# Expert 0's first weight loads ahead of the rank registers, and one 128-slot chunk beside every three 64-slot chunks

## The chip, the cores and the metric

The kernel runs on one core of a Trainium2 chip. The metric is the time of one execution on the device, in microseconds; the median of three runs before the change is 1743.07 us (1742.59 to 1744.09). In the rows PE is TensorE's matmul side and PEld its weight loads, DVE is VectorE, ACT is ScalarE, and SPq is the sequencer of SyncE, which issues all DMA transfers in the order of the program.

## The reference

Two layers of a diffusion backbone over 256 latent tokens of width 1024. Each layer has four token mixers, an output projection and a feed-forward part. In layer 0 that part is a dense SwiGLU; in layer 1, where the change lies, each token goes to two of eight experts:

```python
def swiglu(h, w_gate, w_up, w_down):
    return (jax.nn.silu(h @ w_gate) * (h @ w_up)) @ w_down

def moe_swiglu(h, router_w, w_gate, w_up, w_down):
    ...
    logits = (t @ router_w).astype(jnp.float32)
    top_val, top_idx = lax.top_k(logits, TOP_K)
    top_w = jax.nn.softmax(top_val, axis=-1)
    gate = jnp.sum(jax.nn.one_hot(top_idx, N_EXPERTS, dtype=jnp.float32) * top_w[..., None], axis=1)
    for e in range(N_EXPERTS):
        out = out + gate[:, e:e + 1] * swiglu(t, w_gate[e], w_up[e], w_down[e]).astype(jnp.float32)
```

The hidden width is 3584 and all is in float32. An expert's three matrices are 44 MB, the eight together 352 MB, and every execution reads all of them from the chip's main memory.

## The kernel before

The last stage computes the eight experts from gathered tokens. Each expert has a fixed number of places for tokens (slots). Expert 0 has 128. The seven others are put in order of their load at run time: the fullest, rank 0, gets 128 slots as well, and ranks 1 to 6 get 64 each. Tokens beyond that would go through a loop behind a branch (line 1450).

An expert's hidden width is cut into 14 chunks of 256. A chunk needs three units of weights, 128 x 2048 floats (1 MiB) each: two for the gate and up projections (tile gu) and one for the down projection (tile yd with 128 slots, ys with 64). Each unit is one DMA, issued by `raw_unit` (line 228, or two half transfers in line 223). `raw_unit` walks through a ring of twelve buffers: the old context tile (x), one spare tile, the old parameter tile (prb), a pair of half tiles (cst and prb), and eight raw tiles. A transfer waits until its buffer's last reader is done, and what stands behind it on the queue waits too.

The two kinds of experts are computed in different ways. A 128-slot chunk (`full`) splits each half unit into a high part by ACT (`wh`, line 235) and a remainder by DVE (`wl`, line 237), and PE takes three matmuls in the place of one (`mm3`, lines 245 to 247). There are three pairs of split tiles, and a raw buffer is free when DVE has made the remainder. A 64-slot chunk (`small`) lets PE read the raw buffer as it is (line 1394 for gu, line 1380 for ys), with two halves of the array side by side. In both, ACT applies silu (lines 1332 and 1397), and the down projection of a chunk is computed one chunk later.

Where an expert's weights lie depends on its rank, so seven register loads on SP (line 1436) fetch the order from the tile `ordi`, which DVE writes at the end of the routing. Expert 0's addresses are known when the program is built. Four of its units are loaded during attention (line 1076), and its first four chunks (`HEAD`) stand ahead of everything else.

Behind these, `prep_small` gathers the tokens of ranks 1 to 3 (tile es) and `prep_full` those of rank 0 (tile ef). The loop of lines 1440 to 1447 then runs over the 84 chunks of the 64-slot experts and puts one 128-slot chunk ahead of each for as long as there are any: expert 0's last ten, then the 14 of rank 0. Ranks 4 to 6 are prepared at step 20. A scheduler orders each engine's instructions from this program, with its own model of time.

Of the kernel before, what the change touches and what calls it, by code (L numbers as in the profile page):

```python
# [22 lines left out]
NCH = 14  # L23
# [161 lines left out]
def build(tc, I, out):  # L185
    nc = tc.nc
# [12 lines left out]
    turns = {"raw": 0, "split": 0, "unit": 0}  # L199
# [5 lines left out]
    def ring(kind):  # L205
        i = 2 if kind == "raw" else 3
        n = turns[kind] % sum(w[i] for w in wps)
        turns[kind] += 1
        for w in wps:
            if n < w[i]:  # L210
                return w[0], w[i]
            n -= w[i]

    more = []

    def raw_unit(src, n=2048):
        turns["unit"] += 1
        i = turns["unit"] % (len(more) + sum(w[2] for w in wps))
        if i < len(more):
            r = more[i]()  # L220
            if isinstance(r, list):
                for k, h in enumerate(r):
                    nc.sync.dma_start(h, src[:, k * 1024:k * 1024 + 1024])
                return r
        else:
            wp, bufs = ring("raw")
            r = wp.tile([128, n], F32, tag="raw", bufs=bufs, name="raw")
        nc.sync.dma_start(r, src)
        return r

    def split(r):
# [12 lines left out]
    def mm3(o, wh, wl, rh, rl, start, stop, **kw):  # L244
        PE.matmul(o, wh, rh, start=start, stop=False, **kw)  # L245
        PE.matmul(o, wh, rl, start=False, stop=False, **kw)  # L246
        PE.matmul(o, wl, rh, start=False, stop=stop, **kw)  # L247

    def hilo(hi, lo, src):
        S.activation(hi, src, AF.Copy)  # L250
        V.tensor_tensor(out=lo, in0=src, in1=hi.bitcast(F32), op=ALU.subtract)
# [34 lines left out]
    def adav(l, j, kt, s):  # L286
        return ada[l][:, j * 8 + kt, s:s + 1]
# [16 lines left out]
    def t8(name, dt=F32R, shape=(128, 8, 256)):  # L304
        return a8.tile(list(shape), dt, tag="a8", name=name)
# [10 lines left out]
    def t2(name, shape=(128, 2, 256), dt=F32):  # L316
        return tt("t2", name, shape, dt)
# [426 lines left out]
    def PS():  # L744
        turn[0] += 1
        return PB() if turn[0] % 5 > 2 else pq.tile([128, 512], F32, tag="b0", bufs=3, name="b0")
# [303 lines left out]
    def masks(gm, slots, numbers="iota"):  # L1050

        for t in range(2):
            for i, sl in enumerate(slots):
                j = V.tensor_scalar(gm[:, t, i], C(numbers), sl[t], None, op0=ALU.is_equal)
        return j.ins
# [102 lines left out]
    NR = NE - 1  # L1158
    cap = sm.tile([128, 8], F32, tag="cap", bufs=1, name="cap")
    slr = sm.tile([128, 4, NR], F32, tag="slr", bufs=1, name="slr")  # L1160
    cnti = sm.tile([128, 2], I32, tag="cnti", bufs=1, name="cnti")
    ordi = sm.tile([128, NR], I32, tag="ordi", bufs=1, name="ordi")
# [57 lines left out]
    def slots_of(st, gm, gates):  # L1220

        st.gT = gp.tile([128, 256], F32R, tag="gT", name="gT")
        st.g = sm.tile([128, 1], F32, tag="sg", bufs=8, name="sg")
        ps = PS()
        for t in range(2):
            PE.transpose(ps[:, t * 128:t * 128 + 128], gm[t], ident)
        for t in range(2):
            PE.matmul(ps[:, 256:257], gm[t], gates[t], start=t == 0, stop=t == 1)
        S.activation(st.gT, ps[:, :256], AF.Copy)
        V.tensor_copy(st.g, ps[:, 256:257])  # L1230

    def gather(gm, kts, ps, n):
        for i, kt in enumerate(kts):
            for t in range(2):
                PE.matmul(ps[:, i * n:i * n + n], ht[:, t, kt * 128:kt * 128 + 128], gm[t], start=t == 0, stop=t == 1)

    def prep_full(slots, gates, gm=None):

        st = St()
        if gm is None:  # L1240
            gm = t2("gm", (128, 2, 1, 128))
            masks(gm, [slots])
        gm = [gm[:, t, 0] for t in range(2)]
        e = t8("ef", F32R, (128, 2, 8, 128))
        for k4 in range(2):
            ps = PS()
            gather(gm, range(4 * k4, 4 * k4 + 4), ps, 128)
            for k in range(4):
                kt = 4 * k4 + k
                sh = adav(1, 3, kt, 0)  # L1250
                S.activation(e[:, 0, kt], ps[:, k * 128:k * 128 + 128], AF.Identity, bias=sh)
                V.scalar_tensor_tensor(e[:, 1, kt], ps[:, k * 128:k * 128 + 128], sh, e[:, 0, kt].bitcast(F32), op0=ALU.add,
                                       op1=ALU.subtract)
        st.e = (e[:, 0], e[:, 1])
        slots_of(st, gm, gates)
        return st
# [30 lines left out]
    def split_unit(e, u):  # L1287
        if isinstance(e, int) and e == 0 and u in first:
            r = first[u]
            ws = []  # L1290
            for a in (0, 1024):
                nsplit[0] += 1
                with ExitStack() as st:
                    if nsplit[0] > EARLY:
                        st.enter_context(tc.issue_after(last_mask))
                        st.enter_context(tc.issue_after(sbi))
                    ws.append(split(r[:, a:a + 1024]))
            return ws
        return halves(unit_at(e, u))

    def full(st, e):

        yd = []

        def down(c, g):
            if not yd:
                yd.extend(pq.tile([128, 512], F32, tag=f"yd{i}", name=f"yd{i}") for i in range(2))
            pt = pq.tile([128, 512], F32, tag="tr", bufs=2, name="tr")
            for m in range(2):
                PE.transpose(pt[:, m * 128:m * 128 + 128], g[:, m * 128:m * 128 + 128], ident)  # L1310
            hhl = t2("hhl", (128, 2, 256), F32R)
            hh, hl = hhl[:, 0], hhl[:, 1]
            hilo(hh, hl, pt[:, :256])
            for m, wd in enumerate(split_unit(e, c * 3 + 2)):
                for q in range(2):
                    a = slice(q * 512, q * 512 + 512)
                    h = slice(m * 128, m * 128 + 128)
                    mm3(yd[q], hh[:, h], hl[:, h], wd[0][:, a], wd[1][:, a], c == 0 and m == 0, c == NCH - 1 and m == 1)

        prev = []  # L1320

        def chunk(c):
            eh, el = st.e
            ps = pq.tile([128, 512], F32, tag="gu", bufs=2, name="gu")
            for hf in range(2):
                for k2, w in enumerate(split_unit(e, c * 3 + hf)):
                    for k in range(2):
                        kt = 4 * hf + 2 * k2 + k
                        a = slice(k * 512, k * 512 + 512)
                        mm3(ps, eh[:, kt], el[:, kt], w[0][:, a], w[1][:, a], kt == 0, kt == 7)  # L1330
            g = t1("sg")
            S.activation(g, ps[:, :256], AF.Silu)
            V.tensor_tensor(out=g, in0=g, in1=ps[:, 256:], op=ALU.mult)
            if c:
                down(c - 1, prev.pop())
            prev.append(g)
            if c == NCH - 1:
                down(c, prev.pop())
                st.y = t8("y", F32R, (128, 2, 1024))
                for q in range(2):  # L1340
                    a = slice(q * 512, q * 512 + 512)
                    S.activation(st.y[:, 0, a], yd[q], AF.Copy, scale=st.g)
                    V.scalar_tensor_tensor(st.y[:, 1, a], yd[q], st.g, st.y[:, 0, a].bitcast(F32), op0=ALU.mult,
                                           op1=ALU.subtract)
                scatter_full(st)

        return [lambda c=c: chunk(c) for c in range(NCH)]
# [79 lines left out]
        st0 = prep_full(None, [gate[:, t, 0:1] for t in range(2)], gm0)  # L1427
    more[:] = [old] + [lambda r=r: r for r in spares[:NPRE]] + [old2, old3]
    turns["unit"] = len(more) - 1
    turns["split"] = turns["raw"] = 0  # L1430
    A = full(st0, 0)
    HEAD = 4
    for f in A[:HEAD]:
        f()
    more[:] = [old, lambda: spares[0], old2, old3]
    order = [nc.values_load(ordi[0:1, r:r + 1], engines=(mybir.EngineType.SP,), min_val=1, max_val=7) for r in range(NR)]
    small_sts = prep_small([1, 2, 3])
    st1 = prep_full([slr[:, 2 * t + 1, 0:1] for t in range(2)], [slr[:, 2 * t, 0:1] for t in range(2)])
    A = A[HEAD:] + full(st1, order[0])
    for i in range(6 * NCH):  # L1440
        if i == NCH + 6:
            small_sts += prep_small([4, 5, 6])
        if i < len(A):
            A[i]()
        if i % NCH == 0:
            B = small(small_sts[i // NCH], order[i // NCH + 1], i // NCH == 5)
        B[i % NCH]()
    over = nc.values_load(cnti[0:1, 0:1], min_val=0, max_val=1024)

    with tc.If(over > 512):  # L1450
# [42 lines left out]
```

## Time and profile before

| | us |
|---|---|
| median of the runs (lowest to highest) | 1743.07 (1742.59 to 1744.09) |
| the profiled execution | 1743.34 |
| its span, first to last instruction | 1741.5 |
| PE, matmuls, busy | 1642.9 |
| DVE busy | 856.1 |
| ACT busy | 645.5 |

The page has 525.25 MB of transfers, a mean of 302 GB/s over the span. Its second part cuts the span into 40 equal slices of 43.5 us; a digit is the busy share in tenths. The expert stage begins near 850 us, that is, half-way through these lines.

### The profile page before, as it was taken

What the parts mean: (1) busy time and instruction counts of PE and PEld (TensorE: products, weight loads), DVE (VectorE), ACT (ScalarE), POOL (GpSimd) and SP (SyncE); (2) the same over time, 40 slices, a digit from 0 to 9 for tenths busy, and PEclk for the clock granted to TensorE, in tenths of its full rate; (3) what the DMA queues carried; (4) which work ended last, traced back from release to release, by engine and by line L of the source; (5) the groups of instructions that cost most, each with busy time, mean ns of one, the idle gap of its engine ahead of it and who ended that gap; (6) DMA issues with size and microseconds to landing.
All of it is one profiled execution on the core that took longest, in us unless ns stands there. A gap on an engine that the chain in (4) does not pass through costs nothing.

```text
span 1741.5 us, 28675 instructions
## 1 busy us (share of the span) xinstructions
PE 1642.9 (94%) x11648; PEld 1245.3 (72%) x11648; DVE 856.1 (49%) x1446; ACT 645.5 (37%) x1026; POOL 32.1 (2%) x31
## 2 busy tenths in 40 slices
PE   7999999999999999999999999999999887888886
PEld 4897899999999999989775566566655443444443
DVE  3546676797666666566665555555541110110101
ACT  4534564444454444455664444444430000000000
POOL 0100000000000000000100000000000000000000
PEclk9999999999999999999999999999999999999999
DMA  9425456777644666654579999999999999999997
GB/s 377 158 96 194 141 199 225 291 271 303 245 153 165 222 253 241 224 217 168 199 278 377 381 359 386 390 350 398 381 367 415 419 418 419 418 419 418 420 418 289
DMA packets 77900, 525.25 MB, mean 302 GB/s; under 512 B 9024, under 2 KB 9152, under 8 KB 18240
## 3 DMA queue, kind: packets, MB, share of 16 engines
q1 hardware_dynamic: 77760, 523.33, 77.0%
q8 instruction: 94, 1.54, 0.3%
q14 instruction: 46, 0.38, 0.1%
HBM read 522.25 MB, written 1.05 MB: 300 GB/s over the span
## 4 chain that ended last, share of the span: by engine, by line
PE 73%; DMA 21%; DVE 3%; ACT 2%; issue 1%; POOL 0%; SPq 0%; DVEq 0%; ACTq 0%; POOLq 0%
DMA raw<-in_moe 13%; PE gu L246 9%; PE gu L245 9%; PE gu L247 9%; PE gu L1394 8%; DMA prb<-in_moe 4%; PE acc L246 4%; PE acc L245 4%; PE acc L247 4%; PE ys L1380 3%; DMA x<-in_moe 2%; PE w L245 2%; PE w L247 2%; PE w L246 2%; PE yd L246 1%; PE yd L245 1%
## 5 line engine op out<-in xcount | busy, mean ns | idle before, releaser
L237 DVE TENSOR_TENSOR wl<-raw,wh 128x1024 fp32r<-128x1024 f32 x304 | 370.0, 1224 | 187.8 <-ACT wh L235 181.9
L235 ACT ACTIVATE wh<-raw 128x1024 fp32r<-128x1024 f32 x304 | 319.9, 1059 | 304.8 <-PE gu L246 148.0
L1394 PE MATMUL gu<-raw,es 128*64 128x256 f32 x2048 | 256.8, 385 | 33.3 <-DMA raw<-in_moe 33.3
L245 PE MATMUL gu<-fh,wh 128*128 128x256 f32 x896 | 254.1, 284 | 0.0
L247 PE MATMUL gu<-fh,wl 128*128 128x256 f32 x896 | 251.3, 281 | 0.0
L246 PE MATMUL gu<-fl,wh 128*128 128x256 f32 x896 | 250.9, 280 | 0.0
L1394 PEld LDWEIGHTS gu<-raw,es 128*64 128x64 f32 x2048 | 144.8, 136 | 120.4 <-issue 39.5
L1397 ACT ACTIVATE sg<-gu 64x256 f32<-64x256 f32 x84 | 31.7, 377 | 427.1 <-PE gu L1394 426.6
L1398 DVE TENSOR_TENSOR sg<-sg,gu 64x256 f32<-64x256 f32 x84 | 35.7, 425 | 276.5 <-ACT sg L1397 275.9
L245 PEld LDWEIGHTS gu<-fh,wh 128*128 128x128 f32 x896 | 168.1, 188 | 4.7 <-issue 4.7
L246 PEld LDWEIGHTS gu<-fl,wh 128*128 128x128 f32 x896 | 168.6, 188 | 2.7 <-issue 2.7
L247 PEld LDWEIGHTS gu<-fh,wl 128*128 128x128 f32 x896 | 168.8, 189 | 1.8 <-issue 1.6
L246 PE MATMUL acc<-hl,wh 128*128 128x256 f32 x448 | 124.5, 283 | 0.0
L245 PE MATMUL acc<-hh,wh 128*128 128x256 f32 x448 | 123.8, 283 | 0.0
L247 PE MATMUL acc<-hh,wl 128*128 128x256 f32 x448 | 120.3, 283 | 0.0
L1380 PE MATMUL ys<-raw,hs 128*64 128x512 f32 x400 | 96.0, 599 | 14.8 <-DMA raw<-in_moe 14.0
L246 PE MATMUL gu<-wl,ef 128*128 128x512 f32 x224 | 93.1, 415 | 3.8 <-DVE wl L237 3.7
L245 PE MATMUL gu<-wh,ef 128*128 128x512 f32 x224 | 92.2, 412 | 0.0
L247 PE MATMUL gu<-wh,ef 128*128 128x512 f32 x224 | 88.0, 393 | 0.0
L246 PEld LDWEIGHTS acc<-hl,wh 128*128 128x128 f32 x448 | 85.7, 191 | 0.0
L245 PEld LDWEIGHTS acc<-hh,wh 128*128 128x128 f32 x448 | 85.6, 191 | 0.0
L247 PEld LDWEIGHTS acc<-hh,wl 128*128 128x128 f32 x448 | 83.3, 191 | 0.0
(450 smaller groups left out, 2549.4 us busy)
## 6 DMA issues: line engine op xcount, KB each, us to landing
raw<-in_moe SPq DMA_DIRECT2D x223, 1024.0 KB, 12.3
raw<-in_ffn SPq DMA_DIRECT2D x84, 1024.0 KB, 4.8
spare<-in_moe SPq DMA_DIRECT2D x31, 1024.0 KB, 10.4
x<-in_moe SPq DMA_DIRECT2D x28, 1024.0 KB, 12.6
prb<-in_moe SPq DMA_DIRECT2D x27, 1024.0 KB, 8.7
rx<-in_ada SPq DMA_DIRECT2D x19, 1024.0 KB, 5.0
raw<-in_ada SPq DMA_DIRECT2D x18, 1024.0 KB, 4.9
prb<-in_moe SPq DMA_DIRECT2D x27, 512.0 KB, 10.1
```

The lines of the kernel that those rows point to most:

```text
L235: S.activation(hi, r, AF.Copy)
L237: V.tensor_tensor(out=lo, in0=r, in1=hi.bitcast(F32), op=ALU.subtract)
L245: PE.matmul(o, wh, rh, start=start, stop=False, **kw)
L246: PE.matmul(o, wh, rl, start=False, stop=False, **kw)
L247: PE.matmul(o, wl, rh, start=False, stop=stop, **kw)
L1380: PE.matmul(yd[0][64 * q:64 * q + 64, :], h[:, m * 64:m * 64 + 64], rs[m][:, q * 512:q * 512 + 512], start=c == 0 and m == 0, stop=c == NC ...
L1394: PE.matmul(ps[64 * q:64 * q + 64, :256], st.e[:, kt], rs[k // 2][:, a:a + 256], start=kt == 0, stop=kt == 7, tile_position=(0, 64 * q))
L1397: S.activation(g[64:], ps[:64, :256], AF.Silu)
L1398: V.tensor_tensor(out=g[64:], in0=g[64:], in1=ps[64:, :256], op=ALU.mult)
```

## The change

The diff does two things. The register loads are placed behind the issue of the last weight transfer of the four head chunks (`newest`), and the ring of raw buffers starts at another place. And the loop turns round: every step has its 64-slot chunk, and every third step adds one 128-slot chunk from the list A; rank 0 is prepared at step 28, where expert 0's chunks end, and ranks 4 to 6 at step 36. With 24 chunks in the list, the last 128-slot chunk now goes with step 71 of 0 to 83; before it went with step 23.

```diff
-        nc.sync.dma_start(r, src)
+        newest[:] = [nc.sync.dma_start(r, src).ins]
...
-    turns["split"] = turns["raw"] = 0
+    turns["split"], turns["raw"] = 0, 3
...
-    order = [nc.values_load(ordi[0:1, r:r + 1], engines=(mybir.EngineType.SP,), min_val=1, max_val=7) for r in range(NR)]
+    with tc.issue_after(newest[0]):
+        order = [nc.values_load(ordi[0:1, r:r + 1], engines=(mybir.EngineType.SP,), min_val=1, max_val=7)
+                 for r in range(NR)]
     small_sts = prep_small([1, 2, 3])
-    st1 = prep_full([slr[:, 2 * t + 1, 0:1] for t in range(2)], [slr[:, 2 * t, 0:1] for t in range(2)])
-    A = A[HEAD:] + full(st1, order[0])
+    A = A[HEAD:]
     for i in range(6 * NCH):
-        if i == NCH + 6:
+        if i == 2 * NCH:
+            st1 = prep_full([slr[:, 2 * t + 1, 0:1] for t in range(2)], [slr[:, 2 * t, 0:1] for t in range(2)])
+            A += full(st1, order[0])
+        if i == 2 * NCH + 8:
             small_sts += prep_small([4, 5, 6])
-        if i < len(A):
-            A[i]()
         if i % NCH == 0:
             B = small(small_sts[i // NCH], order[i // NCH + 1], i // NCH == 5)
         B[i % NCH]()
+        if i % 3 == 2 and A:
+            A.pop(0)()
```

The built programs stand in the same order up to the end of the routing, but for SP. In the rows of order below, line numbers of the changed kernel are 1 or 2 higher.

On SP, around the register loads (tile ordi), before: ten units of expert 0 stand ahead of the loads, behind the four of line 1076.

```order
L223 DMA prb_5372<-in_moe 128x1024
L1076 DMA spare<-in_moe 128x2048 x3
L228 DMA raw<-in_wout 128x2048 x3
L223 DMA cst<-in_moe 128x1024
L228 DMA prb_5372<-in_moe 128x2048
L228 DMA raw<-in_moe 128x2048 x3
L228 DMA spare<-in_moe 128x2048
L228 DMA raw<-in_moe 128x2048 x4
L1436 TENSOR_LOAD ordi
L1436 ISA x2
```

The same place in the changed kernel:

```order
L1077 DMA spare<-in_moe 128x2048 x3
L229 DMA raw<-in_wout 128x2048 x3
L229 DMA raw<-in_moe 128x2048 x7
L1438 TENSOR_LOAD ordi
L1438 ISA x2
```

And the first transfers behind its loads:

```order
L229 ISA
L229 DMA spare<-in_moe 128x2048
L229 ISA
L229 DMA prb_5372<-in_moe 128x2048
L224 ISA
L224 DMA cst<-in_moe 128x1024
L224 ISA
L224 DMA prb_5372<-in_moe 128x1024
```

The seven raw transfers of the head chunks now stand together ahead of the loads; the spare tile, the parameter tile and the two half tiles have moved behind them and get a 64-slot expert's weights.

On ACT, two chunk pairs in the mixed stretch, before. L1332 and L1397 are the silu of a 128-slot and of a 64-slot chunk, L235 the splits, six to a 128-slot chunk.

```order
L1332 ACTIVATE sg<-gu 128x256
L250 ACTIVATE hhl<-tr 128x256
L1397 ACTIVATE sg<-gu 64x256
L235 ACTIVATE wh<-raw 128x1024 x6
L1332 ACTIVATE sg<-gu 128x256
L250 ACTIVATE hhl<-tr 128x256
L1397 ACTIVATE sg<-gu 64x256
```

The same engine in the changed kernel, one group:

```order
L1333 ACTIVATE sg<-gu 128x256
L1398 ACTIVATE sg<-gu 64x256 x2
L251 ACTIVATE hhl<-tr 128x256
L1398 ACTIVATE sg<-gu 64x256
L236 ACTIVATE wh<-raw 128x1024 x6
L1333 ACTIVATE sg<-gu 128x256
```

Between two 128-slot chunks there are now three 64-slot chunks, and the six splits of a 128-slot chunk stand together behind the third of them.

## Rows read from the trace of the kernel before

**Rows 1.** The page: busy time of PE, and DMA in 40 slices.

```profile
PE 1642.9 (94%) x11648; PEld 1245.3 (72%) x11648; DVE 856.1 (49%) x1446; ACT 645.5 (37%) x1026; POOL 32.1 (2%) x31
...
DMA  9425456777644666654579999999999999999997
```

**Rows 2.** Busy time by stretch: us, each engine (instructions), granted clock, DMA.

```profile
core 0: us, PE busy (x) PEld busy (x) DVE busy (x) ACT busy (x) POOL busy (x), PEclk, DMA share, GB/s
853.00:890.00 37.00, 37.00 (x183) 31.08 (x181) 28.52 (x33) 28.85 (x42) 0.00 (x0) 1.00 0.68 252
890.00:905.00 15.00, 15.00 (x95) 10.64 (x95) 8.28 (x17) 7.41 (x15) 0.00 (x0) 1.00 0.46 167
905.00:1280.00 375.00, 368.73 (x1888) 231.07 (x1889) 208.19 (x256) 173.86 (x223) 0.00 (x0) 1.00 0.97 379
1280.00:1371.00 91.00, 89.06 (x639) 49.21 (x639) 20.95 (x51) 9.43 (x20) 0.00 (x0) 1.00 0.97 396
1371.00:1725.00 354.00, 290.87 (x2018) 150.24 (x2018) 43.51 (x118) 19.39 (x49) 0.00 (x0) 1.00 1.01 418
```

**Rows 3.** Waits of the SP queue, 905 to 1280: us, times, longest.

```profile
SPq L228 <- DVE wl L237: 109.6, 49, 5.0
SPq L228 <- PE gu L1394: 68.6, 26, 5.2
```

**Rows 4.** The same, 1371 to 1725.

```profile
SPq L228 <- DMA raw<-in_moe: 133.1, 68, 2.7
...
SPq L228 <- PE ys L1380: 2.1, 8, 0.4
```

**Rows 5.** The chain at the end: start, us, the last weight transfer.

```profile
1706.03 19.85 DMA x<-in_moe
```

**Rows 6.** SP queue: the wait before the register loads, the loads, later issues.

```profile
SPq L1436 <- DVE cnti L1208: 17.0, 1, 17.0
...
L1436 SPq TENSOR_LOAD <-ordi x7: 262/263/467, 848.6 to 852.2; - x7
...
868.67 18.00 SPq L228 DMA_DIRECT2D raw<-in_moe  x6
```

**Rows 7.** ACT in order of time: silu of single 64-slot chunks (start, us).

```profile
953.35 0.38 ACT L1397 ACTIVATE sg<-gu 64x256 f32<-64x256 f32 x1
...
969.88 0.38 ACT L1397 ACTIVATE sg<-gu 64x256 f32<-64x256 f32 x1
...
1036.57 0.38 ACT L1397 ACTIVATE sg<-gu 64x256 f32<-64x256 f32 x1 [3.33 <-PE gu L1394]
...
1073.71 0.38 ACT L1397 ACTIVATE sg<-gu 64x256 f32<-64x256 f32 x1 [1.50 <-PE gu L1394]
...
1174.59 0.38 ACT L1397 ACTIVATE sg<-gu 64x256 f32<-64x256 f32 x1 [1.50 <-PE gu L1394]
...
1189.90 0.38 ACT L1397 ACTIVATE sg<-gu 64x256 f32<-64x256 f32 x1 [1.50 <-PE gu L1394]
...
1336.94 0.38 ACT L1397 ACTIVATE sg<-gu 64x256 f32<-64x256 f32 x1 [5.21 <-PE gu L1394]
1342.53 0.38 ACT L1397 ACTIVATE sg<-gu 64x256 f32<-64x256 f32 x1 [5.21 <-PE gu L1394]
...
1476.47 0.38 ACT L1397 ACTIVATE sg<-gu 64x256 f32<-64x256 f32 x1 [7.58 <-PE gu L1394]
1483.95 0.38 ACT L1397 ACTIVATE sg<-gu 64x256 f32<-64x256 f32 x1 [7.11 <-PE gu L1394]
```

**Rows 8.** Busy time by stretch, four short stretches (columns as in rows 2).

```profile
1060.00:1064.00 4.00, 3.71 (x9) 0.99 (x10) 3.63 (x5) 0.00 (x0) 0.00 (x0) 0.57 0.60 248
...
1180.00:1200.00 20.00, 19.60 (x105) 13.07 (x104) 12.65 (x14) 9.81 (x12) 0.00 (x0) 1.00 1.01 417
1240.00:1260.00 20.00, 19.19 (x101) 12.08 (x98) 12.23 (x14) 11.07 (x14) 0.00 (x0) 1.00 1.02 410
1300.00:1340.00 40.00, 38.83 (x284) 21.11 (x284) 7.91 (x21) 2.95 (x7) 0.00 (x0) 1.00 1.01 414
```

More of the change, by code (lines that the diff above doesn't have):

```diff
@@ L214, in build @@
     more = []
+    newest = []
     def raw_unit(src, n=2048):
```

## Prediction

> **What bounds the kernel now.** I read the page first for where the time lies, then the busy time by stretch, then the waits of the SP queue in two stretches, then single instructions for prices. The page [rows 1] shows TensorE (PE) busy 94% of the span, which by itself says too much, and a DMA line that is low in the middle and then 9 to the end. The table by stretch [rows 2] splits that up. From 905 to 1280 us, where each 128-slot chunk stands beside one 64-slot chunk, PE is busy 368.73 of 375 us and DMA moves 379 GB/s. From 1371 to 1725, where only 64-slot chunks are left, PE is busy 290.87 of 354 us and DMA moves 418 GB/s. The SP queue says which of the two is the bound. In the first stretch its waits are for VectorE's (DVE) splits and for PE, that is, for buffers to come free: 109.6 and 68.6 us are the longest [rows 3]. In the second it waits for earlier transfers, 133.1 us, and for PE only 2.1 us [rows 4]. So the kernel is first bound by PE, with DMA partly idle, and then by DMA, with PE idle for 63 of 354 us. The two idle times lie in different stretches, and the change mixes them.
>
> The weights left after 905 us, from rows 2: 375 x 379 + 91 x 396 + 354 x 418 GB/s = 142.1 + 36.0 + 148.0 = 326.1 MB. A unit is 128 x 2048 x 4 bytes = 1.049 MB, so these are 311 of the 336 units (8 experts, 14 chunks, 3 units each), and 25 had landed by 905. The last landing is at 1725.9 (issued at 1706.03, 19.85 us under way), and a tail of 15.6 us follows it [rows 5].
>
> **The change part by part.** *The start.* Before, SP issued 4 + 10 units of expert 0 ahead of the register loads; now 4 + 7, because the units behind the fourth chunk belong to a 64-slot chunk whose address is in a register. Three units, 7.5 us of transfer at 418 GB/s, move behind the loads. The loads start at 848.6, after a wait of 17.0 us for the routing, and the last starts at 852.2 [rows 6]; that doesn't move, since its producer on DVE stands where it stood. I cost the move at nothing. The cover is the hole behind the loads: one raw unit goes out at once, the others wait for buffers of the first four chunks up to 886 (the six of 868.67 take 18.00 us, [rows 6]), and DMA moves only 252 GB/s from 853 to 890 [rows 2]. In the new order the first four units behind the loads find their buffers free (spare, the two pieces of the parameter tile, the eighth raw), and the eight after them wait for the same releases as before. Both kernels have 23 units issued at about 886 (before: 14, then two raw, the x tile and the six). Without that cover the move would cost its 7.5 us. The new ring start (raw turn 3) only swaps which raw buffers these seven units take; no PE work depends on it before 849.
>
> From 890 on there is a gain. Before, the next consumer is a 128-slot chunk behind the preparation of the second 128-slot expert, and DMA falls to 167 GB/s for 15 us [rows 2]: 2.5 MB. Now three 64-slot chunks come first, which free three units each in 5.6 us. At 412 GB/s it would be 6.2 MB, 3.5 units more. I take 3 (bounds 0 and 3.5): 28 landed at 905, 308 left, 323.0 MB.
>
> *The spreading.* A 64-slot chunk costs PE 5.59 us when nothing holds it (1336.94 to 1342.53) and comes every 7.48 us when DMA does (1476.47 to 1483.95) [rows 7]. A pair takes 15.31 us (1174.59 to 1189.90) to 16.53 us (953.35 to 969.88), so its 128-slot chunk costs 9.7 to 10.9 us. Before, a pair's 6.29 MB at 418 would take 15.05 us: PE is later. Now a group is three 64-slot chunks and one 128-slot chunk: PE 16.8 + 9.7 to 10.9 = 26.5 to 27.7 us, DMA 12.58 MB, 30.1 us at 418. DMA is later by 2.4 to 3.6 us. So what is late next is the weight stream, from about 905 to the end, and the sum is bytes over rate.
>
> The rate beside splits: three unhindered stretches of the mixture and just behind it give 417, 410 and 414 GB/s [rows 8]. I take 412 (bounds 400 and 418). The last 128-slot chunk goes with slot 71 of 84, so 12 chunks of 64 slots stay behind it: 36 units, 37.7 MB at 418, 90.3 us. The other 285.3 MB at 412 take 692.4 us. Together 782.7 us: the last landing moves from 1725.9 to 1687.7.
>
> *What is moved.* The preparation of the second 128-slot expert and that of ranks 4 to 6 now stand beside the end of expert 0 and a scatter, within about two groups. Before, the two pairs around expert 0's end took 37.1 us (1036.57 to 1073.71, [rows 7]) against 31 for two plain ones, so 6 us extra; the pieces that join it are a few microseconds each on PE. That is 10 to 20 us of extra PE work against 5 to 7 us that PE has spare in two groups. Up to some 20 us of transfers are under way at any time (19.85 us from issue to landing, [rows 5]), so most of the rest is hidden, and PE regains it later. Exposed: 0 to 10 us, I take 4. The tail behind the last landing keeps its 15.6 us. DMA issues are as many as before, and the 84 + 24 chunks cost PE what they cost.
>
> *Sum.* 1687.7 + 4 + 15.6 = 1707.3 us of span. The profiled execution has 1743.34 us with a span of 1741.5; the median of the runs is 1743.07, 1.6 above the span. Forecast **1709 us**, 34 us (2.0%) less.
>
> **The rivals.** *The stream never starves.* 28.5 units landed at 905, 418 GB/s throughout, nothing exposed: 322.4 / 0.418 = 771.3; 905 + 771.3 + 15.6 + 1.6 = 1694 us. For it: 417 in one stretch of the mixture. Against it: 410 in another.
>
> *Half of it.* The start gains nothing (311 units) and the mixture runs at 400 GB/s: 288.4 / 0.400 + 90.3 = 811.3; 905 + 811.3 + 4 + 17.2 = 1737 us. For it: PE has only 8 to 12% to spare in a group, and its order is fixed, so every late split delays the 64-slot chunks behind it. With the start's gain kept it is 1730.
>
> *Slower.* The 379 GB/s of the mixture belong to the mixture and not to PE: a 128-slot chunk holds its three buffers until ScalarE and DVE have split them, with only three pairs of split tiles, and the queue issues in order, so everything behind waits. Spread over 72 slots, this would reach the weights that now flow at 418: 285.3 / 0.379 = 752.8; 905 + 752.8 + 90.3 + 4 + 17.2 = 1769 us. It decides below 392 GB/s, where the sum passes 1743. For it: the longest wait of the queue there is on the split [rows 3]. Against it: 410 and 417 within the mixture, and PE that is busy 98%, so the splits wait for PE and not PE for them. The Trainium skill (Perfetto Trace Analysis, opening note and "Identifying the Most-Contended Engine") holds that matmul busy time is a poor measure of how near a kernel is to its limit and wants weight-load time; by it this rival would gain weight, for weight loads are busy 231.07 of 375 us [rows 2]. The pair that takes 15.31 us against 15.05 for its bytes is what keeps it small.
>
> *The clock.* PE will now wait for data through the whole stretch. If it lost clock there, a group would cost 27.1 us over the granted share; at a mean of 0.8, 33.9 us, 3.4 more than DMA's 30.5, in 24 groups 81 us: 1790 us. It decides below 0.85. The rows show 0.57 in the four microseconds behind expert 0's end [rows 8], and 1.00 over the 354 us in which PE waited for data 18% of the time [rows 2]; the gaps would be of that second kind. The Trainium skill (TensorE: Matmul & The Clock Gate, "Why this matters for your kernels") warns of idle gaps between bursts of matmuls, since they take the array back to half rate; the gaps of the last stretch didn't do that [rows 2].
>
> *Nothing happens*: some wait in the new order that I don't see eats the gain: 1743.
>
> **How the numbers follow.** Forecast 0.57, no starving 0.20, half 0.12, slower by rate 0.06, slower by clock 0.02, nothing 0.03. The range goes from 1694 to 1734: it takes in the best case and most of the half case (rate bound 400 with the start kept, 1730) and leaves out the slower ones. About 0.2%, 3.5 us, is what a measurement of this kernel can tell from no change: faster 0.89, the same 0.03, slower 0.08.
>
> **What would show it.** Right: between 905 and the end DMA at 405 GB/s or more throughout, the SP queue's waits on earlier transfers and not on splits, PE busy less than 95% in the mixture, 128-slot chunks every 30 to 31 us, the last landing near 1690. At the start: the seven raw transfers ahead of the register loads, the loads at about 848, and no PE wait for a weight before 890. Wrong: a longer wait for routing or a first 64-slot chunk without data (the start), SP waits on DVE above 100 us with DMA under 395 GB/s (the slower rival), a granted clock under 0.9, or a hole of over 10 us around the end of expert 0 (the moved preparations).

## The result, and the profile after

The changed kernel takes 1705.84 us (median of four runs, 1704.32 to 1706.75), the kernel before beside it 1743.58 us (1742.59 to 1745.09). The ratio is 0.9782 with a 95% interval of 0.9765 to 0.9799: 38 us less, where 34 had been forecast (1709 us). The profiled execution of the changed kernel has a span of 1702.5 us and took 1704.32 us.

The page of the changed kernel, busy time of TensorE (PE) and DMA in 40 slices, now of 42.6 us:

```profile
PE 1637.2 (96%) x11648; PEld 1248.4 (73%) x11648; DVE 854.0 (50%) x1446; ACT 645.2 (38%) x1026; POOL 32.2 (2%) x31
...
DMA  9425346778744566654479999999999999999996
GB/s 374 171 100 199 136 174 219 276 278 300 268 170 161 198 248 242 246 186 168 173 298 380 420 418 419 419 418 419 416 418 420 418 417 419 419 419 418 419 418 259
```

PE is busy 1637.2 us, 1642.9 in [rows 1]; its share has grown because the span has shrunk. What changed is the last line: from the 23rd slice to the last but one DMA is level at 416 to 420 GB/s.

Busy time by stretch, changed kernel (us, each engine with its instructions, granted clock, DMA share, GB/s):

```profile
core 0: us, PE busy (x) PEld busy (x) DVE busy (x) ACT busy (x) POOL busy (x), PEclk, DMA share, GB/s
853.00:890.00 37.00, 37.00 (x183) 29.99 (x182) 26.71 (x34) 26.80 (x41) 0.00 (x0) 1.00 0.82 313
890.00:905.00 15.00, 15.00 (x110) 9.33 (x110) 5.46 (x9) 4.75 (x8) 0.00 (x0) 1.00 0.87 308
905.00:1280.00 375.00, 366.11 (x2195) 217.62 (x2192) 141.34 (x222) 109.58 (x162) 0.00 (x0) 1.00 1.01 417
1280.00:1600.00 320.00, 302.25 (x1818) 179.14 (x1815) 120.38 (x178) 92.69 (x126) 0.00 (x0) 0.98 1.01 419
1600.00:1686.00 86.00, 76.20 (x530) 40.45 (x530) 14.93 (x37) 6.39 (x16) 0.00 (x0) 0.98 0.98 406
```

In the stretch from 905 to 1280, which moved 379 GB/s before [rows 2], DMA moves 417, with PE nearly as busy as it was. The 406 of the last stretch is its end, where fewer and fewer transfers are left (400 GB/s from 1675 to 1680, 247 from there to 1686); the last lands at 1685.6.

Waits of the SP queue from 905 to 1280, changed kernel (us, times, longest):

```profile
SPq L229 <- DMA raw<-in_moe: 63.7, 37, 3.1
SPq L229 <- PE gu L1395: 60.4, 29, 5.6
SPq L229 <- PE tr L1374: 35.3, 13, 5.3
SPq L229 <- DVE wl L238: 32.9, 14, 3.5
```

The wait for earlier transfers, which led behind 1371 in [rows 4] and is not among the queue's waits from 905 to 1280 before, is now the longest single line, and the 109.6 us for the splits [rows 3] are 32.9. Added up over all lines of the view, the waits for buffers (PE and DVE, 162.7 us) still exceed those for transfers (127.9 us), so the waits alone don't settle which of the two is the bound. The transfer times of the raw tiles say more. From 905 to 1280, time from issue to landing, the kernel before and then the changed one:

```profile
raw<-in_moe SPq DMA_DIRECT2D x91, 1024.0 KB, 7.4
```

```profile
raw<-in_moe SPq DMA_DIRECT2D x101, 1024.0 KB, 17.4
```

A unit takes 2.5 us at 418 GB/s, so 7.4 us are about three units under way at a time and 17.4 us about seven: while the queue waits for a buffer, DMA still has work. The chain at the end of the changed kernel (start, us) closes with the same transfer as in [rows 5], 40 us earlier:

```profile
1665.66 19.96 DMA x<-in_moe
```

### The profile page after: what moved, and what is told of

Its sections match the earlier page's. It is cut to its first block, busy times and chain, and to the rows that moved or that the text cites. A ratio compares the mean times of both kernels' runs of the same rounds, so it can differ in the third digit from the quotient of the medians.

```text
span 1702.5 us, 28623 instructions
## 1 busy us (share of the span) xinstructions
PE 1637.2 (96%) x11648; PEld 1248.4 (73%) x11648; DVE 854.0 (50%) x1446; ACT 645.2 (38%) x1026; POOL 32.2 (2%) x31
## 4 chain that ended last, share of the span: by engine, by line
PE 76%; DMA 19%; DVE 3%; ACT 1%; issue 1%; SPq 0%; POOL 0%; DVEq 0%; ACTq 0%; POOLq 0%
PE gu L1395 11%; DMA raw<-in_moe 9%; PE gu L247 9%; PE gu L246 9%; PE gu L248 9%; PE ys L1381 5%; DMA prb<-in_moe 5%; PE acc L247 4%; PE acc L246 4%; PE acc L248 4%; DMA x<-in_moe 2%; PE w L246 2%; PE w L248 2%; PE w L247 2%; PE yd L247 1%; DMA spare<-in_moe 1%
## 5 line engine op out<-in xcount | busy, mean ns | idle before, releaser
L238 DVE TENSOR_TENSOR wl<-raw,wh 128x1024 fp32r<-128x1024 f32 x368 | 446.3, 1223 | 221.8 <-ACT wh L236 215.3
L236 ACT ACTIVATE wh<-raw 128x1024 fp32r<-128x1024 f32 x368 | 384.8, 1057 | 330.5 <-PE gu L247 149.8
L1395 PE MATMUL gu<-raw,es 128*64 128x256 f32 x1488 | 181.3, 383 | 5.0 <-DMA raw<-in_moe 4.8
L1395 PEld LDWEIGHTS gu<-raw,es 128*64 128x64 f32 x1488 | 105.5, 137 | 64.5 <-issue 11.2
L1381 PE MATMUL ys<-raw,hs 128*64 128x512 f32 x424 | 103.6, 603 | 7.3 <-DMA raw<-in_moe 6.1
L246 PE MATMUL gu<-wh,ef 128*128 128x512 f32 x224 | 93.4, 418 | 8.2 <-ACT wh L236 8.2
L248 PE MATMUL gu<-wh,ef 128*128 128x512 f32 x224 | 90.3, 403 | 0.0
## 6 DMA issues: line engine op xcount, KB each, us to landing
raw<-in_moe SPq DMA_DIRECT2D x223, 1024.0 KB, 17.4
```

The costliest lines, as they stand in the source:

```text
L236: S.activation(hi, r, AF.Copy)
L238: V.tensor_tensor(out=lo, in0=r, in1=hi.bitcast(F32), op=ALU.subtract)
L1381: PE.matmul(yd[0][64 * q:64 * q + 64, :], h[:, m * 64:m * 64 + 64], rs[m][:, q * 512:q * 512 + 512], start=c == 0 and m == 0, stop=c == NC ...
L1395: PE.matmul(ps[64 * q:64 * q + 64, :256], st.e[:, kt], rs[k // 2][:, a:a + 256], start=kt == 0, stop=kt == 7, tile_position=(0, 64 * q))
```

## The experiments

**The loop alone.** The loop of the changed kernel; the two lines at the start are those of before:

```diff
-    turns["split"], turns["raw"] = 0, 3
+    turns["split"] = turns["raw"] = 0
-    with tc.issue_after(newest[0]):
-        order = [...]
+    order = [...]
```

> The changed loop alone: one 128-slot chunk per three 64-slot chunks, but the register loads and the start of the raw ring as before. The order of SP stands as in the changed kernel either way: seven raw transfers of the head chunks, the register loads, then the first units of a 64-slot expert. So the theory (the gain is the mixing, the two lines at the start do nothing) expects the changed kernel's time, 1706 us within 3. Rival (the start carries part of it, about three units, as the prediction had it): 3 to 8 us more, 1709 to 1714.

Measured: 1703.98 us, ratio to before 0.9768 (0.9755 to 0.9782). The changed kernel, run again later, gave 0.9776 (0.9763 to 0.9790). The loop is the whole gain. It also brings the new order on SP with it: here too seven raw transfers stand ahead of the register loads and the spare tile is the first behind them.

**The start alone.** The same two edits in the loop of before.

> The start alone: raw ring from the fourth buffer and the register loads behind the last head transfer, with the loop of before (128-slot and 64-slot chunks in pairs, then 64-slot chunks alone). Theory: as before, 1743 us within 3.5, PE bound from 905 to 1280 at about 380 GB/s. Rival (the start is worth three units by itself): 1735 to 1738.

Measured: 1743.53 us, ratio 0.9997 (0.9988 to 1.0006). Its mixture is that of [rows 2]:

```profile
905.00:1280.00 375.00, 368.75 (x1888) 230.34 (x1886) 206.19 (x255) 171.91 (x220) 0.00 (x0) 1.00 0.96 378
```

The two lines give nothing by themselves. The three units that the prediction credits to the start are not tested by this: with the old loop ten units of expert 0 stand ahead of the register loads, as before, and the move behind the loads and the three 64-slot chunks that come first belong to the loop.

**PE made cheaper in pairs.** This is the run that tells a slow mixture from a busy PE. The kernel before, unmixed, with one matmul of three taken out of 128-slot chunks:

```diff
     mm3(ps, eh[:, kt], el[:, kt], ...)
+    # behind expert 0's first four chunks:
+    PE.matmul(o, wh, rh, start=start, stop=False)
+    PE.matmul(o, wh, rl, start=False, stop=stop)
```

> The kernel before, in pairs, but 128-slot chunks behind the first four take two matmuls in place of three; the third matmul (remainder of the tokens by high part of the weights) is left out. Splits, transfers and buffers stay. PE saves about 2.8 us in each of 24 chunks. Theory (379 GB/s in the mixture was PE's doing): a pair costs PE 12.5 to 13.7 us against 15.05 us for its bytes, DMA comes to 405 to 418 GB/s, about 311 units from 905 on take 780 to 805 us, and the time is 1703 to 1728 us. Rival (the rate belongs to the mixture, its splits and its queue): DMA stays near 379 GB/s up to the last 128-slot chunk and the time stays at 1738 to 1744 us.

Measured: 1706.89 us, ratio 0.9781 (0.9766 to 0.9796), the changed kernel's ratio. Its stretch from 905 to 1280, then the longest of SP's waits there and its wait for the splits:

```profile
905.00:1280.00 375.00, 356.31 (x1930) 204.08 (x1931) 218.96 (x291) 177.61 (x234) 0.00 (x0) 0.99 1.01 417
```

```profile
SPq L228 <- DMA raw<-in_moe: 112.1, 61, 3.0
...
SPq L228 <- DVE wl L237: 17.4, 15, 4.7
```

Transfers, splits, split tiles and the order of chunks are those of before, with even more DVE work in the stretch (218.96 us against 208.19), and DMA goes at 417 GB/s. So the 379 GB/s belonged to PE. The 109.6 us of waiting for splits [rows 3] were a wait for PE at one remove, since a split needs one of three pairs of tiles and a pair comes free when PE has read it. With PE busy 57.0 us less over the whole run (1585.9 in place of 1642.9), 2.4 us for each of 24 chunks, they fall to 17.4.

**PE made cheaper in the changed kernel.** The same matmul taken out of the changed kernel.

> The changed kernel, and 128-slot chunks behind the first four take two matmuls in place of three; the third (remainder of the tokens by high part of the weights) is left out. PE saves 2.8 us in each of 24 chunks, 67 us in all. Theory (from 905 us on the weight stream is the bound): DMA stays at 417 to 419 GB/s, PE only idles more, and the time is 1699 to 1707 us. Rival (PE, busy 98% from 905 to 1280, still sets the time): 67 us less for PE alone, at least 30 us of it in the time, 1640 to 1675 us.

Measured: 1704.84 us, ratio 0.9769 (0.9754 to 0.9784): no difference, although PE has 288 matmuls less to do and is busy 45.1 us less, 1592.1 in place of 1637.2 (I had put it at 67). The page's line, and the stretch:

```profile
PE 1592.1 (93%) x11360; PEld 1193.9 (70%) x11360; DVE 850.7 (50%) x1446; ACT 643.5 (38%) x1026; POOL 32.0 (2%) x31
```

```profile
905.00:1280.00 375.00, 348.19 (x2110) 192.86 (x2108) 140.33 (x226) 109.79 (x164) 0.00 (x0) 0.98 1.01 419
```

PE is busy 18 us less in the stretch and DMA goes on at its rate. The queue's waits there move from buffers (162.7 us, now 45.4) to transfers (127.9, now 250.4) and the time stays. PE's busy 366 of 375 us in the changed kernel was no sign that it set the time.

**Fewer bytes.** The other direction: the changed kernel with 44 MB less to load. It leaves out the second half of every 64-slot chunk's down unit and uses the first half twice, so the number of matmuls stays and the values are not those of the layer.

```diff
-            r = raw_unit(unit_at(e, c * 3 + 2))
-            rs = r if isinstance(r, list) else [r[:, 0:1024], r[:, 1024:2048]]
+            r = raw_unit(unit_at(e, c * 3 + 2)[:, 0:1024], half=True)
+            rs = [r, r]
```

> The changed kernel, but of the down unit of every 64-slot chunk only the first half is loaded and used twice, 44.0 MB less in 84 chunks; the number of matmuls stays. Theory (the stream is the bound, with PE close behind): a group has 10.5 units, 11.0 MB, 26.3 us at 418 GB/s, against 26.5 to 27.7 us of PE, so PE becomes the bound in the mixture at about 27.1 us a group, and the last twelve 64-slot chunks take 6.3 us each by their 2.62 MB: 24 x 27.1 + 12 x 6.3 = 726 us, with some 15 us of moved preparations and 17 us of tail from 905 on: 1655 to 1680 us, PE busy 98% or more in the mixture. Rival (PE or the mixture is the bound already): 1698 to 1706 us.

Measured: 1657.71 us, ratio 0.9496 (0.9481 to 0.9510). At 418 GB/s the bytes alone are 105 us; 48 us of that came, and then PE was the bound:

```profile
905.00:1280.00 375.00, 372.59 (x2271) 223.39 (x2269) 142.78 (x226) 110.31 (x164) 0.00 (x0) 1.00 0.96 382
1280.00:1600.00 320.00, 315.11 (x1962) 188.44 (x1960) 128.01 (x195) 94.70 (x131) 0.00 (x0) 1.00 0.99 395
...
1160.00:1200.00 40.00, 40.00 (x243) 25.71 (x241) 24.60 (x44) 17.58 (x29) 0.00 (x0) 1.00 0.62 227
```

This run also shows what the moved preparations can cost when DMA has no lead. In 40 us around the preparation of rank 0 DMA falls to 227 GB/s, about 17 us of transfer at 400, and SP waits 16.4 us in one piece for a buffer that PE has yet to read:

```profile
SPq L227 <- PE ys L1386: 16.4, 1, 16.4
```

In the changed kernel the same 40 us have:

```profile
1160.00:1200.00 40.00, 37.90 (x232) 24.96 (x230) 22.27 (x46) 15.14 (x27) 0.00 (x0) 1.00 1.01 419
```

**A closer mixture.** One 128-slot chunk per two 64-slot chunks:

```diff
-        if i % 3 == 2 and A:
+        if i % 2 == 1 and A:
```

> The changed kernel with one 128-slot chunk per two 64-slot chunks; rank 0 is prepared at step 20, ranks 4 to 6 at step 28. A group is 9 units, 22.6 us at 418 GB/s, against 20.9 to 22.1 us of PE: DMA is later by only 0.5 to 1.7 us. Theory (whoever is later in the group sets the time, and small holes are made good by the transfers under way): DMA at 410 to 418 GB/s from 905 on and 1706 us within 5. Rival (the slack of 2.4 to 3.6 us in a group of three is what carries the moved preparations and the late splits): the mixture falls to 395 to 405 GB/s and the time is 1712 to 1724 us.

Measured: 1711.05 us, ratio 0.9804 (0.9790 to 0.9817), 6 us above the 1705.1 of the changed kernel's second set of runs. Neither expectation holds quite: the time is at the edge of the first (1711), the 409 GB/s of the mixture lie between the two.

```profile
905.00:1280.00 375.00, 368.72 (x2133) 225.57 (x2131) 167.36 (x243) 133.16 (x187) 0.00 (x0) 1.00 1.00 409
...
1120.00:1160.00 40.00, 39.34 (x243) 24.38 (x243) 20.89 (x41) 15.42 (x25) 0.00 (x0) 1.00 0.93 374
```

8 GB/s less than in the changed kernel over 375 us are 3.0 MB, 7 us. More than half of that is in one place: the preparation of rank 0, where 374 in place of 418 GB/s for 40 us are 1.8 MB, 4.2 us. The rest is from 1200 to 1280, with and just behind the preparation of ranks 4 to 6: 408 and 397 GB/s in its two halves, 3.0 us. From 1040 to 1120 and from 1160 to 1200 DMA runs at 418 to 419. So a group with 0.5 to 1.7 us to spare still runs at the bytes' rate, and pays when something extra comes. That it has less in stock then is my reading; the median from issue to landing is 11.6 us there, 17.4 in the changed kernel.

**The start, by its head chunks.** Two runs with fewer chunks of expert 0 ahead of all others (`HEAD = 4` set to 3 and to 2).

> The changed kernel with three head chunks of expert 0 in place of four: two raw units fewer ahead of the register loads (nine units landed by 853 in place of eleven or so), and the first 64-slot chunks about 9 us earlier. Between 853 and 905 the changed kernel moves 313 and 308 GB/s with PE busy throughout; a 128-slot chunk frees three buffers in 9 to 10 us (about 315 to 340 GB/s), a 64-slot chunk in 5.6 us. Theory (the start is bound by how fast PE frees buffers): DMA comes to 370 to 418 GB/s from 853 to 905, one to three units more have landed by 905, and the time is 1696 to 1703 us. Rival (the units queued ahead of the register loads are what counts at the start): two units fewer, 5 us more, 1707 to 1711 us.

> The changed kernel with two head chunks of expert 0 in place of four: six units ahead of the register loads. By the theory that PE's order frees buffers, DMA could run at 400 to 418 GB/s from 856 on, 20 units from 853 to 905, 26 by 905: as the changed kernel, 1702 to 1708 us, since what the earlier 64-slot chunks win the shorter queue ahead of the loads loses. By the rival (units ahead of the loads count and nothing else): five units fewer, 12 us more, 1714 to 1720 us.

Measured: 1703.80 us (ratio 0.9771, 0.9758 to 0.9784) with three, 1702.41 us (0.9759, 0.9746 to 0.9773) with two. Against the changed kernel's 0.9776 (0.9763 to 0.9790) that is no difference with three, and at most a small gain with two, which the intervals don't settle. For three I had expected 1696 to 1703, for two 1702 to 1708. Three stretches of the start, changed kernel:

```profile
770.00:809.00 39.00, 38.87 (x305) 35.62 (x304) 27.48 (x58) 21.86 (x40) 3.87 (x3) 1.00 0.38 142
809.00:853.00 44.00, 39.74 (x309) 33.56 (x308) 26.61 (x78) 20.98 (x44) 5.21 (x5) 0.96 0.43 168
853.00:905.00 52.00, 52.00 (x291) 39.32 (x291) 32.17 (x42) 31.55 (x48) 0.00 (x0) 1.00 0.83 312
```

The same with three head chunks:

```profile
770.00:809.00 39.00, 38.87 (x306) 35.91 (x304) 29.39 (x58) 22.59 (x42) 3.17 (x2) 1.00 0.45 170
809.00:853.00 44.00, 39.76 (x305) 33.59 (x304) 25.79 (x80) 21.85 (x47) 5.21 (x5) 0.96 0.14 49
853.00:905.00 52.00, 52.00 (x292) 37.05 (x292) 27.70 (x34) 27.14 (x41) 0.00 (x0) 1.00 0.92 371
```

Earlier 64-slot chunks do free buffers sooner: 371 GB/s against 312, 3.1 MB more from 853 to 905. But fewer units stand ahead of the register loads, and 4.1 MB fewer came from 770 to 853. The two cancel.

**Both at once.** Three head chunks, with the fourth's units still issued ahead of the register loads and its matmuls behind the first three 64-slot chunks:

```diff
-    HEAD = 4
+    HEAD = 3
     for f in A[:HEAD]:
         f()
+    for u in (9, 10, 8):
+        pre[u] = raw_unit(unit_at(0, u))
```

> The changed kernel with three head chunks, but the units of the fourth are still issued ahead of the register loads (seven raw transfers, as in the changed kernel); only its matmuls move behind the first three 64-slot chunks. Theory (both count at the start, the units ahead of the loads and how early the 64-slot chunks free buffers): 168 GB/s from 809 to 853 as in the changed kernel and 350 GB/s or more from 853 to 890 as with three head chunks, two units more landed by 905, 1697 to 1702 us. Rival (the units of the fourth chunk hold three of twelve buffers until about 905, so the transfers behind the loads find fewer): no gain, 1703 to 1707 us.

Measured: 1716.30 us, ratio 0.9839 (0.9825 to 0.9852), 11 us above the changed kernel and worse than either expectation.

```profile
853.00:890.00 37.00, 37.00 (x203) 28.70 (x203) 23.18 (x31) 24.27 (x39) 0.00 (x0) 1.00 0.69 256
890.00:905.00 15.00, 15.00 (x93) 9.11 (x89) 5.54 (x8) 4.21 (x6) 0.00 (x0) 1.00 0.35 121
```

The issues on SP at the end of that hole (start, us):

```profile
891.65 0.33 SPq L229 DMA_DIRECT2D raw<-in_moe  x1
901.57 0.33 SPq L229 DMA_DIRECT2D raw<-in_moe  x1
902.11 0.33 SPq L229 DMA_DIRECT2D x<-in_moe  x1
902.65 0.33 SPq L229 DMA_DIRECT2D spare<-in_moe  x1
903.18 0.53 SPq L229 DMA_DIRECT2D prb<-in_moe  x1
903.91 0.33 SPq L224 DMA_DIRECT2D cst<-in_moe  x1
904.46 0.33 SPq L224 DMA_DIRECT2D prb<-in_moe  x1
```

And its waits from 853 to 905:

```profile
SPq L229 <- DVE wl L238: 28.9, 5, 9.3
```

The rival named the held buffers and thought of three in twelve. What it missed is the order. SP comes to a raw buffer of the ring that is not yet split, waits for it, 9.3 us the last time, and the transfers behind stand in the queue: at the end of that wait five of them go out within 3 us, so their buffers were free by then. The same with two head chunks and the third's units ahead:

> Two head chunks, and the third's units issued ahead of the register loads (four raw transfers there), its matmuls behind the first three 64-slot chunks. Theory: two to three units more ahead of the loads than with two head chunks alone, near 400 GB/s from 853 to 905 as there: two units more by 905, 1696 to 1701 us. Rival (held buffers): 1702 to 1706 us.

Measured: 1707.79 us, ratio 0.9797 (0.9784 to 0.9811), 5 us more than with two head chunks alone and above both expectations. Its longest wait from 853 to 905 is another, 12.2 us for DVE's sg (9.0 with two head chunks alone), so the account by a held raw buffer is shown for three head chunks only. The changed kernel itself, beside these two:

> The changed kernel once more, unaltered, beside the two variants of its start on the same chip: 1703 to 1707 us.

Measured: 1705.10 us (1702.54 to 1707.88), ratio 0.9776 as above. No order of the start that I tried is clearly better than the changed kernel's.

## Why the prediction was right, step by step

**The bound.** The argument was that PE sets the pace in the mixture, DMA behind it, and that mixing thinner turns that round. Three runs show it: with PE cheaper the pairs reach 417 GB/s and the changed kernel's time; with PE cheaper the changed kernel gains nothing; with fewer bytes it gains 48 us and PE becomes the bound. Not all signs of being right came as stated. PE was to be busy less than 95% in the mixture; it was 97.6% up to 1280 and 94.5% from there to 1600. And the queue's waits are on transfers only in part, as said above.

**The start** was costed at nothing and credited with three units by 905. The bytes behind 905 in the changed kernel are 375 x 417 + 320 x 419 + 86 x 406 GB/s = 325.4 MB, 310 units, where 311 were left before and 308 were forecast. So it gained one unit, not three, and the time is 5 us more than forecast by this term. Two steps were mis-sized. The hole behind the loads was to cover all three units that moved behind them; from 853 to 890 DMA moves 313 GB/s where it moved 252 [rows 2], which is 2.2 units, so 0.8 of a unit was still missing at 890. And the rate from 890 to 905 was taken as 412 GB/s; the row has 308, against 167 before, which wins 2.0 units in place of three. At 905 the queue was still waiting for buffers of the head chunks. From 853 to 905, changed kernel:

```profile
SPq L229 <- DVE wl L238: 25.5, 6, 6.2
SPq L229 <- PE gu L1395: 7.1, 3, 3.5
```

The free buffers behind the loads were as described (spare, the parameter tile, the halves, one raw, issued from 854.24 on). No run parts the move behind the loads from the loop, so what the move costs by itself stays open.

**The group.** Forecast: PE 26.5 to 27.7 us, DMA 30.1 to 30.5, 128-slot chunks every 30 to 31 us. ACT's silu of 128-slot chunks, changed kernel, first and last of two runs of groups (start, us):

```profile
916.35 0.38 ACT L1333 ACTIVATE sg<-gu 128x256 f32<-128x256 f32 x1 [4.34 <-PE gu L248]
...
1113.93 0.38 ACT L1333 ACTIVATE sg<-gu 128x256 f32<-128x256 f32 x1 [1.65 <-PE gu L248]
...
1273.32 0.38 ACT L1333 ACTIVATE sg<-gu 128x256 f32<-128x256 f32 x1 [0.30 <-PE gu L248]
...
1597.69 0.38 ACT L1333 ACTIVATE sg<-gu 128x256 f32<-128x256 f32 x1 [0.30 <-PE gu L248]
```

The later eleven groups take 324.4 us, 29.5 each, near the forecast. The first seven take 197.6 us, 28.2 each, less than the 30.1 their bytes need: they use 84 units while 417 GB/s bring 78.6, so PE eats into the units that stand loaded in the buffers. From 905 to 1280 PE waits 8.7 us in all, so 28.2 us is about what a group costs it there (one rank's scatter is among them), more than the 26.5 to 27.7 of the forecast. The slack was 1.9 us a group, not 2.4 to 3.6. While the stock lasts, PE and DMA are both near their limits.

**The rate** was taken as 412 GB/s for the mixture, from short stretches of 410, 414 and 417. It was 417 to 419. That is the term that gave back what the start lost: 285.3 MB at 418 are 682.5 us in place of 692.4, 9.9 us less. The mistake was to take the stretches of 410 and 414 for unhindered ones and their rate for a price of the splits: from 1240 to 1260 SP waits 9.7 us for PE and 7.5 us for splits, and from 1300 to 1340 it waits 29.0 us for PE and for no split. The last landing is at 1685.6, forecast 1687.7.

**The moved preparations** were to show 4 us. They show none: DMA stays at 416 to 419 GB/s around them, while three groups of 128-slot chunks take 101 us from 1145.54 to 1246.69, some 16 us more than three of 28.2. The loaded units and the transfers under way hid all of it, as argued. The run with fewer bytes, whose DMA has no lead, pays for them, and the closer mixture pays a part.

**The tail** took 16.9 us behind the last landing, 1.3 more than the 15.6 of before.

Together: 1707.3 forecast, +5 for the start, -9.9 for the rate, -4 for the preparations, +1.3 for the tail and +2.5 for the thin end of the stream (406 GB/s over the last 86 us) make 1702.2, where the span is 1702.5. The mechanism carried the forecast; that the number is 3 us off (1709 against 1705.84) and not more is in part luck, since the terms that were too hopeful and those that were too cautious nearly cancel.

**The rivals.** "Never starves" (1694) had the rate and the preparations right and the start wrong. "Half" and "slower by rate" fell with the 417 GB/s of the mixture, and the run of pairs with two matmuls shows why they had to: the 379 were not the mixture's. That PE, busy 366.11 of 375 us, is not the bound was shown by taking 288 of its matmuls and 45.1 us of its busy time away; its weight loads are busy 217.62 us there, 13 less than before. The Trainium skill (Perfetto Trace Analysis, "Identifying the Most-Contended Engine") warns against matmul busy time as a measure of the limit; this trace agrees with the warning, at 366.11 of 375 us, though not with the use that the rival made of it. The same page ("Optimization Strategy") says that a kernel with several regimes may gain when they are interleaved; here that is 38 us. "The clock" fell too: its mean by stretch is 0.98 to 1.00, near its upper level of 2.4 GHz. It dips in a few places behind gaps of PE, as here, where PE is idle for 2.1 of 5 us and then runs 5 us at a mean of 0.67, between the levels of 1.2 and 2.4 GHz. DMA goes on at 423 and 415 GB/s:

```profile
1555.00:1560.00 5.00, 2.89 (x14) 1.28 (x11) 2.44 (x3) 2.69 (x4) 0.00 (x0) 0.99 1.02 423
1560.00:1565.00 5.00, 5.00 (x16) 3.93 (x16) 3.02 (x4) 2.56 (x3) 0.00 (x0) 0.67 1.01 415
```

## What to carry to other kernels

Where one stretch is bound by an engine and another by the weight stream, lay them over each other so thinly that the stream is the later of the two in every group, with something to spare for extra work: here the 1.9 us of 30.1 that a group had left were enough, while the closer mixture, costed at 0.5 to 1.7 us of 22.6, held the rate elsewhere and lost 6 us, mostly at the extra work. Whether a busy engine is the bound is shown best by making it cheaper. In a trace the time from issue to landing is a sign (7.4 or 17.4 us here); whether the queue waits for transfers or for buffers is a weaker one, since the changed kernel ran at the full rate with 162.7 us of waits for buffers. And a unit that is loaded early but used late can cost more than its buffer: in the run with three head chunks the queue, which issues in order, stopped at it, and five transfers stood behind.

## What the runs showed of the hardware

From 905 to 1280 the stream goes at 417 GB/s with PE busy 98% and DVE busy 141 of 375 us, 90 of them on the splits, in the changed kernel, and at the same 417 with DVE busy 219 us, 164 of them on the splits, in the pairs with two matmuls. I had expected to pay 1 to 2% for the splits. The Trainium skill (DMA: Bandwidth & Descriptors, "Where 436 GB/s comes from") holds that the main memory's limit per core, about 358 GB/s, which it works out as half of a stack's 716 for two cores, binds such loads, and not the 435 GB/s of the fabric. This kernel runs on one core; it holds 417 and 419 GB/s over stretches of 375 and 320 us, and the measurement decides.
